# Delta-rule levels with two chunks in one stationary tile, one of them reversed; mixer tiles from a free list; modulation steps placed in VectorE's expected waits

## The chip, the cores and the metric

One NeuronCore of a Trainium2 chip runs the whole program; the other cores are idle. The metric is the device time of one execution in microseconds (us). The kernel before takes 2743.76 us, the median of three runs (2742.51 to 2744.02). About 0.2% (5.5 us) is what a measurement of this kernel can tell from no change.

The engines are named as in the profile: PE is TensorE (PEld its weight loads), DVE is VectorE, ACT is ScalarE, POOL is GpSimd, SP is the engine whose queue issues most DMAs. Each engine takes its instructions in the order in which the program lists them for it.

## The reference: what is computed

One layer of a streaming encoder on 512 prompt frames and 64 sample frames, model width 2048, all in float32. Modulation vectors come from a condition vector (`mod = silu(c) @ w_ada + b_ada`, six vectors of 2048 for prompt and sample). A modulated RMSNorm feeds one input projection; its columns go to two kinds of mixers, four heads of gated linear attention (GLA) and eight heads of gated DeltaNet (GDN); both are exact causal recurrences over the frames. Their gated, normalised outputs are joined and projected back to 2048, then a convolutional feed-forward network follows. What the change touches is the delta rule:

```python
def gdn_step(s, blk):
    '''Gated delta rule: S_t = a_t (I - b_t k_t k_t^T) S_{t-1} + b_t k_t v_t^T, o_t = S_t^T q_t.'''
    ...
    lower = jnp.where(strict, jnp.einsum('bhid,bhjd->bhij', kb, k) * decay, 0.0)
    rhs = jnp.concatenate([v * beta, kb * jnp.exp(big_g)[..., None]], axis=-1)
    sol = lax.linalg.triangular_solve(eye + lower, rhs, left_side=True, lower=True,
                                      unit_diagonal=True)
```

For each head and chunk of frames a unit lower triangular matrix has to be inverted (or solved with). The kernel uses chunks of 128 frames, four per head for the prompt; the 64 sample frames of all eight heads are handled as one more "head" whose four tiles hold two heads each.

## The kernel before, in words

**Stages.** The head normalises x, computes the first two modulation vectors and begins the projection of six of the column blocks. Then, from about 170 us of the span, the mixer stage: `gdn_heads` and `gla_heads` run the remaining 50 column blocks of the input projection one after the other (`in_tile`, 16 products each; a product, `mm6`, is six matmuls of 288 columns, because each float32 operand is split into a high and a low part, `wh`/`wl` and `hh`/`hl`). Then comes the first half of the output projection, over the GDN outputs (16 blocks of 8 products, operands from `load_o`, lines 1515 to 1524), its second half over the GLA outputs (again 16 blocks of 8), then the feed-forward part, which does not concern this change. The split of a weight block into `wh` (ACT) and `wl` (DVE) is emitted with a raised priority.

**Jobs and ticks.** The mixers run as Python generators beside the projection. After each product `tick` (line 624) advances a modelled clock by 0.795 us and lets one job do its next step (`job_step`, line 638). A job yields after a step until the modelled time of its chain of operations (`chain`, kept by `charge`, line 359) is reached, so its matmuls land between the products on PE at a place where their inputs should be there. On DVE and ACT the operations of jobs and of the modulation follow each other in the order of emission (`behind`, line 380); only the weight splits float. The same tick adds 0.72 to a credit and spends it on steps of the late modulation vectors (`ada_blocks`, line 1131): 512 DVE operations of 128x512 (`acc<-aw,ct,acc` and `acc<-xr,ct,acc`), whose weights arrive by 512 KB DMAs; it does so only where the modelled DVE is less than 1 us behind.

**The delta rule, line 189.** `gdn` builds the decay matrices `dl` and `du` (128 x 4 chunks x 128) with ACT and POOL (`affine_select` cuts the triangle), the four matrices `a` (PE, lines 249 to 251), and inverts them: `inverse16` (line 410) first inverts the 16x16 diagonal blocks on DVE, with the blocks moved to 32 lanes and back by DMAs through DRAM (`d0`, `d1`); then the levels 16, 32 and 64 join blocks of that size (lines 266 to 293). A level has two products with a DVE step behind each. `u` and `t` are the inverse and its transpose so far. Every product takes the 128x128 tile of one chunk as the stationary operand and moves 64 columns past it, so a level has four matmuls per product; level 64 uses 64x64 corners:

```python
        for s in (16, 32):
            ...
            for b in range(4):
                T.matmul(ps[:, b * 64:(b + 1) * 64], a[:, b], uh[:, b * nq:(b + 1) * nq], start=True, stop=True)
```

Between levels four transposes renew `t`. After the levels the four chunks are run in order with the state `st`. The GLA levels (`gla`, line 450) already hold two chunks in one stationary tile: the second of a pair is stored with its frames reversed, so that the strict lower triangle of one and the upper triangle of the other share a 128x128 tile, and 128 columns move past it.

**Narrow vectors.** `narrow` (line 1194) computes the decays and gates of all heads for the whole sequence, a chain of short operations on all engines at the start of the mixer stage; cumulative sums are matmuls with triangular constants (`tri`, `tri2`) and last rows with `l127` and `l63`.

**Mixer tiles.** `_MixPool` (line 2348) has 29 tiles of 128x512 in three rings: 17 `m`, 8 `qkv` and 4 `gt`. A new tile takes the oldest of its ring. `fewer` (line 607) holds a GLA job or the sample job back while more than one delta-rule job runs.

A helper records each timed operation, so its line stands for many: in the profile L2272 and L2297 are DVE and ACT operations of jobs and of tasks or splits, L2316 matmuls and L2312 transposes of jobs, L2330 POOL operations; L675 and L677 are the projection's matmuls with `wh` and `wl`.

Of the kernel before, what the change touches and what calls it, by code (L numbers as in the profile page):

```python
# [77 lines left out]
def _shape_constants():  # L78
# [18 lines left out]
    m["l127"] = np.repeat((r == 127)[:, None], P, 1) * 1.0  # L97
    m["l63"] = np.repeat((r == 63)[:, None], P, 1) * 1.0
# [10 lines left out]
NARROW = ("tri", "tri2", "l127", "l63")  # L109


class Kern:
    def __init__(self, tc, ctx, i, o):
# [7 lines left out]
        self.table, self.floating, self.last_of = None, False, {}  # L121
# [22 lines left out]
    def m(self, tag="m", w=512):  # L144
        return self.mp.tile([P, w], F32, tag=tag, name=self.name(tag))

    def m4(self, tag="m"):
        return self.m(tag).rearrange("p (b t) -> p b t", b=4)
# [40 lines left out]
    def gdn(self, qF, kF, x, gain, hcols, gb, s0, s_out, o_put, last_level):  # L189
# [18 lines left out]
        dl, du = self.m4(), self.m4()  # L208
# [5 lines left out]
        self.pool.affine_select(du, du, pattern=[[0, 4], [1, P]], compare_op=ALU.is_ge, fill=0.0, base=0, channel_multiplier=-1)  # L214
        self.pool.affine_select(dl, dl, pattern=[[0, 4], [-1, P]], compare_op=ALU.is_gt, fill=0.0, base=0, channel_multiplier=1)
        if pair:
            self.pool.memset(du[0:64, :, 64:P], 0.0)
# [5 lines left out]
        kT = self.m4()  # L223
# [23 lines left out]
        a = self.m4()  # L247
# [15 lines left out]
        half = lambda x, s, h: flat(x).rearrange("p (n h s) -> p n h s", h=2, s=s)[:, :, h]  # L263
        row4 = lambda x, s: x.rearrange("p (n s) -> p n s", s=s)
        for s in (16, 32):
            uh = half(u, s, 1)
            nq = 64 // s
            ps = self.bank()
            for b in range(4):
                T.matmul(ps[:, b * 64:(b + 1) * 64], a[:, b], uh[:, b * nq:(b + 1) * nq], start=True, stop=True)  # L270
            four = lambda x: x.rearrange("p (b n i) -> p b n i", b=4, i=s)
            V.tensor_tensor(four(pm), four(ps[:, :256]), walk(c[f"p{s}"], 0, (0, 4), (1, nq), (0, s)), op=ALU.mult)
# [4 lines left out]
            V.tensor_tensor(uh, uh, row4(ps[:, :256], s), op=ALU.add)  # L277
            yield from self.hop()
            if s < last_level:
                A.activation(half(t, s, 0), half(self.transpose4(u), s, 0), AF.Copy)  # L280
                yield from self.hop()
        if last_level == 64:
            ps = self.bank()
            for b in range(4):
                T.matmul(ps[:64, b * 64:(b + 1) * 64], a[64:, b, :64], u[64:, b, 64:], start=True, stop=True)
            V.tensor_copy(pm[:64], ps[:64, :256])
            yield from self.hop()
            ps = self.bank()
            for b in range(4):
                T.matmul(ps[:64, b * 64:(b + 1) * 64], t[:64, b, :64], pm[:64, b * 64:(b + 1) * 64], start=True, stop=True)  # L290
            V.tensor_copy(u[:64, :, 64:], ps[:64, :256].rearrange("p (b n) -> p b n", b=4))
            yield from self.hop()
# [46 lines left out]
        if not pair:  # L339
            nc.sync.dma_start(s_out, st)  # L340
# [2053 lines left out]
```

## Time and profile before

| what | value |
|---|---|
| median of three runs | 2743.76 us |
| the profiled execution: its time | 2741.56 us |
| the profiled execution: its span, first to last instruction | 2739.9 us |
| granted PE clock, mean | 0.999 |
| PE busy in the span | 2699.0 us (99%) |
| DVE busy in the span | 2280.0 us (83%) |
| matmuls on PE in the trace | 20404 |
| first matmul of `narrow` | 170.6 us |

The trace is from one execution, 2.2 us faster than the median. A float32 matmul of a job shows as two instructions (two passes), a transpose as one, a projection matmul as one. Matmuls are pipelined, so their busy times overlap, and what one costs is read from the distance between the starts of successive groups in the timeline, not from its duration. In the groups, `out<-in,in` gives the tiles by name without buffer numbers; then the shapes, the count, the busy time, the mean in ns, and the idle time of that engine just before.

### The profile page before, as it was taken

To read this page: it belongs to the slowest core of one execution; us is meant where nothing else is said; L and a number is where in the kernel's file an instruction comes from. 1 tells how busy PE (TensorE), PEld (TensorE's weight loads), DVE (VectorE), ACT (ScalarE), POOL (GpSimd) and SP (SyncE) were. 2 spreads that over 40 slices of the span, in tenths; PEclk is the share of its full clock that TensorE was granted. 3 is DMA by queue.
4 is the path that set the end of the run, shared out by engine and by line. 5 is a ranking of instruction groups with operands and counts; after the bars stand their busy time and mean duration, and the time that the engine had idled before them with its cause. 6 is when DMAs were issued, how large, how long until landed. Compare 5 with 4: busy or idle time off the path is not lost.

```text
span 2739.9 us, 52447 instructions
## 1 busy us (share of the span) xinstructions
PE 2699.0 (99%) x20404; PEld 2632.7 (96%) x20404; DVE 2280.0 (83%) x3691; ACT 1295.7 (47%) x2286; POOL 473.8 (17%) x440
## 2 busy tenths in 40 slices
PE   7999999999999999999999999999999999999998
PEld 5799999999999989999999999999999999999998
DVE  4578887788888898678999999999999976888896
ACT  4245545545644442454545454545454545333453
POOL 0000100001000000001333333333333300000241
PEclk9999999999999999999999999999999999999999
DMA  9985555555565676534464646455655595664762
GB/s 312 344 266 145 152 154 142 148 145 162 168 170 151 177 240 197 148 101 121 138 191 140 188 144 184 149 181 152 179 152 179 151 316 180 209 217 123 238 179 84
DMA packets 645919, 487.61 MB, mean 178 GB/s; under 512 B 66315, under 2 KB 568070, under 8 KB 645670
## 3 DMA queue, kind: packets, MB, share of 16 engines
q1 hardware_dynamic: 632564, 470.77, 57.5%
q10 hardware_dynamic: 13104, 13.47, 1.7%
q8 instruction: 161, 2.64, 0.4%
q14 instruction: 90, 0.72, 0.1%
HBM read 400.12 MB, written 84.04 MB: 177 GB/s over the span
## 4 chain that ended last, share of the span: by engine, by line
PE 89%; DVE 5%; DMA 3%; ACT 1%; issue 1%; SPq 0%; POOL 0%; ACTq 0%; DVEq 0%
PE g L675 19%; PE bank L1785 17%; PE bank L1784 17%; PE bank L1786 17%; PE g L677 9%; PE bank L2316 5%; PE bank L2312 1%; PE bank L675 1%; DVE acc L2297 1%; DVE m L2272 1%; PE bank L904 1%; PE bank L677 1%; DVE wl L1694 0%; DVE wl L2297 0%; PE g L835 0%
## 5 line engine op out<-in xcount | busy, mean ns | idle before, releaser
L1785 PE MATMUL bank<-slot,wh 128*128 128x290 f32 (+1 forms) x3584 | 1067.3, 298 | 0.0
L1784 PE MATMUL bank<-slot,wh 128*128 128x290 f32 (+1 forms) x3584 | 1063.1, 297 | 1.7 <-DVE v L1807 0.6
L1786 PE MATMUL bank<-slot,wl 128*128 128x290 f32 (+1 forms) x3584 | 1060.0, 296 | 1.7 <-DVE wl L1694 1.7
L1786 PEld LDWEIGHTS bank<-slot,wl 128*128 128x128 f32 x3584 | 680.0, 190 | 3.1 <-DVE wl L1694 2.9
L1784 PEld LDWEIGHTS bank<-slot,wh 128*128 128x128 f32 x3584 | 675.4, 188 | 6.3 <-issue 4.7
L1785 PEld LDWEIGHTS bank<-slot,wh 128*128 128x128 f32 x3584 | 676.9, 189 | 0.1
L675 PE MATMUL g<-hh,wh 128*128 128x288 f32 x2048 | 469.5, 310 | 2.2 <-ACT wh L2297 1.3
L1692 ACT ACTIVATE wh<-raw 128x1024 fp32r<-128x1024 f32 (+1 forms) x304 | 280.7, 924 | 348.2 <-PE bank L1785 323.1
L677 PE MATMUL g<-hh,wl 128*128 128x288 f32 x2048 | 439.4, 296 | 2.4 <-DVE wl L1072 2.1
L675 PE MATMUL g<-hl,wh 128*128 128x288 f32 x2048 | 440.6, 296 | 0.9 <-DVE hl L1523 0.6
L1694 DVE TENSOR_TENSOR wl<-raw,wh 128x1024 fp32r<-128x1024 f32 (+1 forms) x304 | 374.6, 1233 | 69.3 <-ACT wh L1692 66.1
L1692 ACT ACTIVATE wh<-s 128x1024 fp32r<-128x1024 f32 (+1 forms) x228 | 210.9, 927 | 298.2 <-PE bank L1785 139.7
L675 PEld LDWEIGHTS g<-hh,wh 128*128 128x128 f32 x2048 | 323.6, 189 | 18.6 <-issue 11.9
L677 PEld LDWEIGHTS g<-hh,wl 128*128 128x128 f32 x2048 | 328.9, 188 | 4.3 <-DVE wl L1072 2.3
L675 PEld LDWEIGHTS g<-hl,wh 128*128 128x128 f32 x2048 | 328.7, 188 | 3.5 <-issue 1.9
L1694 DVE TENSOR_TENSOR wl<-s,wh 128x1024 fp32r<-128x1024 f32 (+1 forms) x228 | 250.4, 1100 | 14.2 <-ACT wh L1692 12.8
L2297 ACT ACTIVATE wh<-raw 128x1024 fp32r<-128x1024 f32 x135 | 143.3, 1062 | 186.0 <-PE g L675 177.6
L2297 DVE SCALAR_TENSOR_TENSOR acc<-aw,ct,acc 128x512 f32<-128x512 f32 x280 | 198.9, 743 | 2.2 <-DMA aw<-in_w_ada_dram 2.2
L1908 POOL TENSOR_TENSOR j<-j,j 128x288 f32<-128x288 f32 (+1 forms) x120 | 186.1, 1557 | 84.0 <-ACT j L1912 81.8
L2297 DVE TENSOR_TENSOR wl<-raw,wh 128x1024 fp32r<-128x1024 f32 x135 | 166.0, 1230 | 16.9 <-ACT wh L2297 14.3
L2297 DVE SCALAR_TENSOR_TENSOR acc<-xr,ct,acc 128x512 f32<-128x512 f32 x200 | 143.0, 744 | 0.0
L1980 DVE TENSOR_TENSOR slot<-bank,slot 128x288 f32<-128x288 f32 x184 | 83.1, 452 | 34.2 <-PE bank L1786 32.9
(330 smaller groups left out, 3274.2 us busy)
## 6 DMA issues: line engine op xcount, KB each, us to landing
raw<-in_w_up_dram SPq DMA_DIRECT2D x176, 512.0 KB
raw<-in_w_in_dram SPq DMA_DIRECT2D x100, 512.0 KB
raw<-in_w_down_dram SPq DMA_DIRECT2D x128, 320.0 KB
slot<-cd SPq DMA_DIRECT2D x140, 288.0 KB
aw<-in_w_ada_dram SPq DMA_DIRECT2D x78, 512.0 KB
cd<-j SPq DMA_DIRECT2D x120, 288.0 KB
xr<-in_w_ada_dram SPq DMA_DIRECT2D x50, 512.0 KB
hraw<-in_w_ada_dram SPq DMA_DIRECT2D x40, 512.0 KB
```

Of the source, the lines that this page charges most:

```text
L675: T.matmul(ps[:, h if bank is None else bank, :n], wh, x[:, h, :n], start=f, stop=False)
L677: T.matmul(ps[:, h if bank is None else bank, :n], wl, ah[:, h, :n], start=False, stop=stop)
L904: T.matmul(ps[32 * k:32 * k + 32, :w], cs[:, k0 + k], got[n][k // per][:, k % per], start=(n == together - 1 + 8 * g + 4 * (1 - mi)), stop ...
L1692: self.nc.scalar.activation(hi, src, AF.Copy)
L1694: self.nc.vector.tensor_tensor(lo, src, hi.bitcast(F32), op=ALU.subtract)
L1784: T.matmul(ps, wh[:, j], hi, start=(c < 3 and j == 0), stop=False, skip_group_check=True)
L1785: T.matmul(ps, wh[:, j], lo, start=False, stop=False, skip_group_check=True)
L1786: T.matmul(ps, wl[:, j], hi, start=False, stop=(j == n - 1), skip_group_check=True)
L1908: minus = lambda out, a, b: G.tensor_tensor(out, a, b, op=ALU.subtract)
L1980: V.tensor_tensor(dst, ps, dst, op=ALU.add)
L2297: r = f(*a, **kw)
L2316: return self.engine.matmul(out, *a, **kw)
```

## The change

The levels now handle a pair of chunks at once. Chunks are stored in the order 0, 2, 1, 3 (the function `slots` that GLA had already used), the chunks in the last two places reversed in time: `gdn_conv` writes q, k and v that way, `narrow` computes its vectors for reversed chunks with reversed triangles (`trir`, `tri2r`, `l0`, `l64`) in more and smaller matmuls, the `affine_select`s become four of half the size, and the outputs are turned back at the end. A reversed chunk's matrix is strictly upper triangular, so the sum of two chunks' matrices (`both`, one new DVE addition) is a full tile without overlap, and `t` holds the two transposed inverses in the same way. A level's product is then two matmuls with 128 moving columns instead of four with 64. Level 64 becomes a level like the others, with the whole 128x128 tile.

`inverse16` inverts the blocks of the reversed chunks in lanes 32 to 47 (lanes 16 to 31 are idle), with three short copies instead of one at its end and one at its start that reverse the lanes, and writes them back with three DMAs instead of one.

Mixer tiles come from one free list of 29; a tile is given back by `drop` when its last reader has been emitted. A job asks for its tiles in advance (`room`) and waits until that many and five more are free; `fewer` is gone. A convolution task waits until the one before has ended (`converting`).

`fill_gap` is called before every timed DVE operation: where the model expects that operation to wait at least 0.5 us for its chain, modulation steps are emitted ahead of it, as far as the credit goes.

```diff
+SPARE = 5
-ADA_BACKLOG, ADA_CREDIT = 1.0, 200.0
+ADA_BACKLOG, ADA_CREDIT, GAP_US = 1.0, 200.0, 0.5
...
+    def room(self, n):
+        while self.mp.spare() < n + SPARE:
+            yield WAIT
+        self.mp.held += n
+        return _Room(n)
...
-        dl, du = self.m4(), self.m4()
+        back, room = room, room or (yield from self.room(5))
+        dl, du = self.m4(room), self.m4(room)
...
-        self.pool.affine_select(du, du, pattern=[[0, 4], [1, P]], compare_op=ALU.is_ge, fill=0.0, base=0, channel_multiplier=-1)
-        self.pool.affine_select(dl, dl, pattern=[[0, 4], [-1, P]], compare_op=ALU.is_gt, fill=0.0, base=0, channel_multiplier=1)
+        for m, op, up in ((du, ALU.is_ge, 1), (dl, ALU.is_gt, -1)):
+            for z, sign in ((slice(0, 2), up), (slice(2, 4), -up)):
+                self.pool.affine_select(m[:, z], m[:, z], pattern=[[0, 2], [sign, P]], compare_op=op, fill=0.0, base=0, channel_multiplier=-sign)
...
-        u, t = yield from self.inverse16(a, gb)
-        pm = dl.rearrange("p b t -> p (b t)")[:, :256]
...
-        for s in (16, 32):
-            uh = half(u, s, 1)
+        pm, both = flat(dl)[:, :256], flat(dl)[:, 256:].rearrange("p (r t) -> p r t", r=2)
+        V.tensor_tensor(both, a[:, 0:2], a[:, 2:4], op=ALU.add)
+        u, t = yield from self.inverse16(a, gb, room)
+        for s in (16, 32, 64):
+            if s > last_level:
+                break
             nq = 64 // s
             ps = self.bank()
-            for b in range(4):
-                T.matmul(ps[:, b * 64:(b + 1) * 64], a[:, b], uh[:, b * nq:(b + 1) * nq], start=True, stop=True)
+            for r in range(2):
+                T.matmul(walk(ps, r * 64, (P, 2), (s, nq), (1, s)), both[:, r],
+                         walk(u, r * P + s, (256 - s, 2), (2 * s, nq), (1, s)), start=True, stop=True)
...
             ps = self.bank()
-            for b in range(4):
-                T.matmul(ps[:, b * 64:(b + 1) * 64], t[:, b], pm[:, b * 64:(b + 1) * 64], start=True, stop=True)
+            for r in range(2):
+                T.matmul(walk(ps, r * 64, (P, 2), (1, 64)), t[:, r], walk(pm, r * 64, (P, 2), (1, 64)), start=True, stop=True)
...
-        if last_level == 64:
-            ps = self.bank()
-            for b in range(4):
-                T.matmul(ps[:64, b * 64:(b + 1) * 64], a[64:, b, :64], u[64:, b, 64:], start=True, stop=True)
...
-        V.tensor_copy(xt, xx.rearrange("p i j -> p j i"))
+        V.tensor_copy(xt[:16], xx[:16].rearrange("p i j -> p j i"))
+        V.tensor_copy(lane[odd, 1], lane[odd, 0][:, ::-1])
+        V.tensor_copy(xx[odd], xt[odd].rearrange("p i j -> p j i"))
         yield from self.until()
-        nc.sync.dma_start(d1.rearrange("w q f -> q w f"), lane)
-        self.moved()
+        nc.sync.dma_start(d1[:, 0:16].rearrange("w q f -> q w f"), lane[:16])
+        for w in range(2):
+            nc.sync.dma_start(d1[w, 16:32], lane[odd, 1 - w])
+        self.moved(3)
...
+    def fill_gap(self):
+        if self.filling or self.floating or self.chain is None:
+            return
+        while self.at_ada >= 1 and self.chain - max(self.free["V"], self.now + HOP_US) >= GAP_US:
+            if not self.ada_step():
+                return
...
-        T.matmul(ps[:, :32], c["tri"], ln[:, :32], start=True, stop=True)
-        T.matmul(ps[:, 32:36], c["tri2"], ln[:, 32:36], start=True, stop=True)
+        for z, n in ((0, ""), (2, "r")):
+            T.matmul(turned(ps, z), c["tri" + n], turned(ln, z), start=True, stop=True)
+            T.matmul(ps[:, 32 + z:34 + z], c["tri2" + n], ln[:, 32 + z:34 + z], start=True, stop=True)
...
+    def drop(self, x):
+        self.free.append(self.place.pop(x.tensor.name))
```

What this moves on the engines is seen in the order of the built programs (a row's name `m_3138` is a mixer tile with its number; `x4` counts equal neighbours). On PE, the first delta-rule job's levels 16 and 32 and its first product of level 64, without the projection's rows between them, before:

```order
L2316 MATMUL bank_3185<-m_3138,m_2702 128x64 x4
L2316 MATMUL bank_3211<-m_2355,m_3137 128x64 x4
L2312 MATMUL bank_3233<-consts_227,m_3138 128x128 x4
L2316 MATMUL bank_3260<-m_3138,m_2702 128x64 x4
L2316 MATMUL bank_3280<-m_2355,m_3137 128x64 x4
L2312 MATMUL bank_3321<-consts_227,m_3138 128x128 x4
L2316 MATMUL bank_3365<-m_3138,m_2702 64x64 x4
```

And now:

```order
L2414 MATMUL bank_3311<-m_3287,m_2377 128x2x64 x2
L2414 MATMUL bank_3351<-m_2377,m_2794 128x2x64 x2
L2410 MATMUL bank_3406<-consts_227,m_3287 128x128 x4
L2414 MATMUL bank_3424<-m_3287,m_2377 128x2x64 x2
L2414 MATMUL bank_3475<-m_2377,m_2794 128x2x64 x2
L2410 MATMUL bank_3498<-consts_227,m_3287 128x128 x4
L2414 MATMUL bank_3531<-m_3287,m_2377 128x2x64 x2
```

Each product has two matmuls of 2x64 columns in place of four of 64; the transposes stay. Over the whole program 144 matmuls of 128x64 and 64 of 64x64 go, and 104 of 128x2x64 come; `narrow` has 17 matmuls instead of 11.

On DVE, around the first level of that job, before:

```order
L2297 TENSOR_TENSOR m_3138<-cm_3077,consts_2028 128x512
L2272 TENSOR_TENSOR m_3147<-bank_3148,m_2731 128x512
L2272 TENSOR_TENSOR m_2732<-bank_3160,m_2732 128x512
L2272 TENSOR_TENSOR qkv_2436<-qkv_2436,m_2442 128x512
L2272 TENSOR_TENSOR m_2355<-bank_3185,consts_2028 128x256
```

And now, with two modulation steps ahead of the level's first DVE step:

```order
L2395 TENSOR_TENSOR m_3287<-cm_3234,consts_2028 128x512
L2395 SCALAR_TENSOR_TENSOR acc_2785<-aw_2818,ct,acc_2785 128x512
L2395 SCALAR_TENSOR_TENSOR acc_2784<-aw_2818,ct,acc_2784 128x512
L2368 TENSOR_TENSOR m_2377<-bank_3311,consts_2028 128x256
L2395 SCALAR_TENSOR_TENSOR acc_2785<-aw_2818,ct,acc_2785 128x512
```

The steps `acc<-aw` that stood behind the level's operations stand ahead of and between them; the last sum of the modulation moves from product 990 of the program to product 952.

On SP, the last writes of the sample frames' GLA outputs (`od_63` to `od_70`, eight of them) and the first loads for the second half of the output projection (`xr<-od`, `raw<-od`). Before, the writes stand among the weights of the first half (`raw<-in_w_out`) and of the modulation (`aw`):

```order
L1341 DMA od_68<-m_12103 256x1x32
L1341 DMA od_70<-m_12103 256x1x32
L582 DMA out_dram<-sl_12535 128x256
L777 DMA raw_12961<-in_w_out_dram 128x8x128
L1520 DMA xr_13352<-od_63 128x576
L1520 DMA xr_13364<-od_65 128x576
L1111 DMA aw_12718<-in_w_ada_dram 128x2x512
L777 DMA raw_13030<-in_w_out_dram 128x8x128
```

And now right ahead of all the loads, the last weights of the first half being issued before them; the row behind is the first block's weights for the second half:

```order
L1431 DMA od_66<-m_12900 256x1x32
L1431 DMA od_68<-m_12900 256x1x32
L1431 DMA od_70<-m_12900 256x1x32
L1616 DMA xr_13374<-od_63 128x576
L1616 DMA raw_13380<-od_64 128x576
L1616 DMA xr_13386<-od_65 128x576
L1616 DMA raw_13392<-od_66 128x576
L1616 DMA raw_13404<-od_68 128x576
L1616 DMA xr_13398<-od_67 128x576
L1616 DMA raw_13416<-od_70 128x576
L1616 DMA xr_13410<-od_69 128x576
L846 DMA raw_13434<-in_w_out_dram 128x8x128
```

The loads are held behind the writes, and the weights behind the loads. The sample job of GLA now ends last: its final transposes stand behind product 995 on PE, with 29 products to go in the first half; before, the last transposes of a mixer job stood behind product 947. On PE the rows ahead of `narrow` and those behind product 995 are the same as before.

More of the change, by code (lines that the diff above doesn't have):

```diff
@@ L302, in gdn @@
         for b in range(4):
-            parts = [(0, P, st)] if not pair else [(0, 64, s0[2 * b]), (64, P, s0[2 * b + 1])]
+            at = b % 2 * 2 + b // 2
+            heads = [2 * b + (n if b % 2 == 0 else 1 - n) for n in range(2)]
+            parts = [(0, P, st)] if not pair else [(0, 64, s0[heads[0]]), (64, P, s0[heads[1]])]
             if parts[0][2] is not None:
@@ L590, in gla @@
             yield
+        for t in ons:
+            self.drop(t, back)
         yield from self.until()
@@ L607, in run_due @@
             self.due.pop(0)[1]()
-    def fewer(self, n):
-        while sum(j[0].__name__ == "gdn" for j in self.jobs) > n:
-            yield WAIT
     def start(self, gen, at=0.0):
@@ L1394, in gdn_samples @@
         x = {}
-        yield from self.fewer(1)
+        room = yield from self.room(8)
         self.put_ready(x, "q", None, 0.0)
@@ L1414, in gla_samples @@
     def gla_samples(self, x):
-        tiles = [self.get_s(n, 256) for n in ("aq", "ak", "ag")]
+        room = yield from self.room(7)
+        tiles = [self.get_s(n, 256, room) for n in ("aq", "ak", "ag")]
         self.moved(3)
@@ L2346, in __getitem__, with __init__ @@
         return st
+class _Room:
+    def __init__(self, n):
+        self.n = n
 class _MixPool:
-    BUFS = {"m": 17, "qkv": 8, "gt": 4}
+    SLOTS = 29
     def __init__(self, tc):
         self.g = tc.tile_pool(name="mp", bufs=1, side="right", reuse_waits="tile")
+        self.free, self.place, self.held = [f"m{n}" for n in range(self.SLOTS)], {}, 0
     def __enter__(self):
```

281 lines of the change are left out of this document (178 added, 103 removed).

## The prediction

> **What bounds the kernel now.** I read the page's busy times and slices first, then the stretches of the stage that changes, then the groups of PE by shape, and last PE's timeline at single groups.
>
> ```profile
> span 2739.9 us, 52447 instructions
> PE 2699.0 (99%) x20404; PEld 2632.7 (96%) x20404; DVE 2280.0 (83%) x3691; ACT 1295.7 (47%) x2286; POOL 473.8 (17%) x440
> PE   7999999999999999999999999999999999999998
> PE 89%; DVE 5%; DMA 3%; ACT 1%; issue 1%; SPq 0%; POOL 0%; ACTq 0%; DVEq 0%
> ```
>
> PE is busy in 99% of the span, and the chain that ended last runs through PE for 89% of it. In stretches (columns: length, then busy time of PE, PEld, DVE, ACT, POOL, the granted clock, DMA share, GB/s), the middle one reaching from the first matmul of `narrow` to the place behind which PE's rows are the same again:
>
> ```profile
> 0.00:170.60 170.60, 149.63 (x1193) 117.51 (x1193) 91.99 (x215) 61.34 (x123) 5.35 (x17) 1.00 0.96 315
> 170.60:1085.00 914.40, 909.05 (x6989) 881.91 (x6989) 777.09 (x1647) 455.40 (x1058) 69.38 (x71) 1.00 0.60 169
> 1085.00:2739.90 1654.90, 1640.33 (x12225) 1633.33 (x12223) 1410.87 (x1830) 778.96 (x1105) 399.06 (x352) 1.00 0.56 169
> ```
>
> In the middle stretch PE idles 914.40 − 909.05 = 5.35 us, at a full clock; DVE is busy for 777.09 us (85%), ACT for 455.40 (50%). So in that stretch the time is what PE's instructions take one behind the other. A job's matmul has no free place there: it stands between two products of the projection, and each us that it takes off PE comes off the end, as long as nothing else takes the place. The first and the last stretch keep their rows on PE, and I let them stand.
>
> **The change part by part.**
>
> *The levels.* These are the groups that go, by shape, and a GLA level for comparison (two instructions for each matmul):
>
> ```profile
> L2316 PE MATMUL bank<-m,m 128*128 128x64 f32 x288 | 36.1, 268 | 0.3 <-DVE m L2297 0.3
> L2316 PE MATMUL bank<-m,m 64*64 64x64 f32 x128 | 10.8, 224 | 0.0
> L2316 PE MATMUL bank<-m 128*128 128x128 f32 x124 | 19.3, 274 | 0.0
> ```
>
> The means of 268 and 274 ns are times from start to end; neighbours overlap, so the price is read between starts. One product of level 32, one of level 64, four plain matmuls of 128 columns, and one GLA level, each with the two rows behind it:
>
> ```profile
> 312.09 1.00 PE L2316 MATMUL bank<-m,m 128*128 128x64 f32 x8
> 312.90 0.51 PE L675 MATMUL g<-hh,wh 128*128 128x288 f32 x2
> 313.24 0.44 PE L675 MATMUL g<-hl,wh 128*128 128x288 f32 x2
> ...
> 319.62 0.68 PE L2316 MATMUL bank<-m,m 64*64 64x64 f32 x8
> 320.23 0.54 PE L675 MATMUL g<-hh,wh 128*128 128x288 f32 x2
> 320.61 0.43 PE L675 MATMUL g<-hl,wh 128*128 128x288 f32 x2
> 320.87 0.43 PE L677 MATMUL g<-hh,wl 128*128 128x288 f32 x2
> ...
> 336.07 1.05 PE L2316 MATMUL bank<-qkv,qkv 128*128 128x128 f32 x8
> 336.87 0.51 PE L675 MATMUL g<-hh,wh 128*128 128x288 f32 x2
> 337.22 0.43 PE L675 MATMUL g<-hl,wh 128*128 128x288 f32 x2
> ...
> 960.87 0.60 PE L2316 MATMUL bank<-m 128*128 128x128 f32 x4
> 961.23 0.51 PE L675 MATMUL g<-hh,wh 128*128 128x288 f32 x2
> 961.58 0.43 PE L675 MATMUL g<-hl,wh 128*128 128x288 f32 x2
> ```
>
> Eight instructions of 64 columns hold PE from 312.09 to 312.90, and the pair behind them needs 0.34 us in place of the 0.26 that an undisturbed pair takes (320.61 to 320.87): 1.15 us up to 313.24. Eight of 128 columns take the same, 336.07 to 337.22 = 1.15. So the price is per instruction, 0.10 us, whether it moves 64 or 128 columns. The GLA level, four instructions of 128 columns in two runs, is what the new product looks like, and it takes 960.87 to 961.58 = 0.71 us. The product of level 64 takes 319.62 to 320.61 = 0.99.
>
> The count: 288 instructions of 128x64 are 36 products (9 jobs, 2 levels, 2 products), 128 of 64x64 are 16 (8 jobs, the sample job has no level 64). All 52 become the GLA form: 36 × (1.15 − 0.71) = 15.8 us, 16 × (0.99 − 0.71) = 4.5 us, together **20.3 us less on PE**. What is new in the form is that the first product of a level fetches its columns in runs of 16, 32 or 64; the old one did too, at 0.10 us an instruction, but there half as many columns were fetched per weight load, so a slower fetch could have been hidden. Bounds: nothing, and for 104 instructions (26 first products of four) a second 0.10 us, 10 us. I take nothing: at level 32 the old form already ran at the price of the plain one.
>
> In the Trainium skill, "TensorE: Matmul & The Clock Gate", section "Back-to-back issue gap", gives an isolated matmul a gap of its columns over 2.4 plus 2.5 ns, so a price by columns. The columns stay the same, 208 × 64 = 104 × 128 = 13,312; by that rule the levels would gain nothing, and it is the third rival below. The rows disagree with it at this size.
>
> *Narrow.* Six more float32 matmuls. Their price here:
>
> ```profile
> 188.62 0.30 PE L1253 MATMUL bank<-cum,xr 128*128 128x36 f32 x2
> 188.76 0.36 PE L1254 MATMUL bank<-cum,xr 128*128 128x4 f32 x2
> 188.98 0.27 PE L1269 MATMUL bank<-consts,cum 128*36 128x128 f32 x1
> ```
>
> Between 0.14 and 0.22 us each, 0.8 to 1.3 us; I take **+1.2**. The rest of `narrow` (about 16 short DVE copies, a constant tile twice as long) lengthens a chain that PE waits for only through `narrow`'s own matmuls, which stand two products later on PE than before; I take nothing, with the bounds of the new waits below.
>
> *DVE, ACT, POOL, DMA of the delta rule.* None of these sets the end; what hides them is PE's 914 us. On DVE each of the nine jobs gains one addition and three short copies and trades the level-64 copies for a masked product and an addition of like size:
>
> ```profile
> L2272 DVE TENSOR_TENSOR m<-m 128x256 f32<-128x256 f32 x56 | 21.0, 417 | 0.0
> L2272 DVE COPY m<-m 32x256 f32<-32x256 f32 x9 | 3.4, 374 | 0.3
> L2297 DVE SCALAR_TENSOR_TENSOR acc<-aw,ct,acc 128x512 f32<-128x512 f32 x280 | 198.9, 743 | 2.2 <-DMA aw<-in_w_ada_dram 2.2
> ```
>
> That is 0.42 + 3 × 0.37 = 1.5 us, for nine jobs 14 us; with 3 us for `narrow`, DVE would have 794 us of work in a stretch of 895, 89% in place of 85%. ACT gets 31 more instructions, POOL 21, SP 18 more small DMAs; all stay far below PE. If the cover went, 17 us of DVE would be the price.
>
> *Modulation steps in the gaps.* The same 512 steps run; those put ahead of a job's operation delay it by up to 0.74 us each if the wait is shorter than the model thought. Queued behind them on DVE are that job's product, the next splits `wl` and, through PE's order, the projection. A step that waits for its own DMA delays all of these; in the trace that came to 2.2 us over 280 steps. PE's waits for DVE in the whole stretch are part of its 5.35 us. So the bounds for new or lost waits in the stage are −5 (all of the old ones go) and +11 (twice as many come on top); I take nothing.
>
> *Mixer tiles, `room`, no `fewer`.* No instruction. Their effect is in the jobs' places: the sample GLA job now ends late, and the second half of the output projection begins 29 products behind its last transposes. A product takes 3 × 0.265 = 0.80 us, so 23 us remain. What has to follow is seen at the same place before (DVE's timeline, then SP's):
>
> ```profile
> 1101.07 0.76 DVE L1523 TENSOR_TENSOR slot<-raw,slot 128x576 fp32r<-128x576 f32 x1 [1.68 <-ACT slot L1522]
> 1101.81 0.94 DVE L2297 SCALAR_TENSOR_TENSOR slot<-g,mod,slot 128x512 f32<-128x512 f32 x2
> 1105.15 1.22 DVE L2297 TENSOR_TENSOR wl<-raw,wh 128x1024 fp32r<-128x1024 f32 x1 [2.40 <-ACT wh L2297]
> 1108.19 0.94 DVE L2297 SCALAR_TENSOR_TENSOR slot<-g,mod,slot 128x512 f32<-128x512 f32 x2 [1.82 <-PE g L677]
> ...
> 1040.03 5.26 SPq L1341 DMA_DIRECT2D od<-m  x8
> ```
>
> Before, the last of the eight operand splits ran at 1101.07 and the first weights were ready at 1106.37, 1.8 us ahead of the first half's end at 1108.19. Now the eight writes take 5.3 us of issue behind the transposes; with about 2 us of ACT and DVE ahead, some 4 us to a first load's split and 8 to 10 for eight splits and the weights (all three estimates from the distances in these rows) that is 19 to 21 us of the 23. I take no wait; the bounds are none and 6 us.
>
> *The sum.* The profiled execution took 2741.6 us: 2741.6 − 20.3 + 1.2 = 2722.5. The median is 2.2 us above the profile, which gives 2724.7; I forecast between the two, **2724 us**.
>
> **The rivals.**
>
> *PE waits take back a part.* DVE is fuller, steps stand ahead of jobs, and the late sample job meets the second half: with 5 to 11 us of new waits from the bounds above, 2729 to 2735. For it speaks that SP's loads now stand right behind the writes; against it that a stage with DVE at 85% left PE idle for only 5.35 of 914 us. Chance 0.17.
>
> *The old waits go too.* These are PE's largest at the start of the output projection, where operands came late:
>
> ```profile
> 998.61 0.52 PE L675 MATMUL g<-hl,wh 128*128 128x288 f32 x2 [0.56 <-DVE hl L1523]
> 1002.00 0.54 PE L675 MATMUL g<-hh,wh 128*128 128x288 f32 x2 [1.35 <-ACT wh L2297]
> ```
>
> The GDN sample job is now done earlier than there, so up to 5 us more may go: 2719. Chance 0.12.
>
> *Columns set the price.* Then only `narrow` counts, 2744 + 1 = 2745, no change. Against it the two 1.15 us above. Chance 0.03; that the pairs are not formed at all is ruled out by the order.
>
> *Slower: the late sample job starves the second half.* One mechanism: writes, loads, splits and weights of the second half stand in one line behind the GLA sample job's last transposes. If that line takes L us, PE waits L − 23. It turns the gain of 19 into a loss of over 5.5 us from L = 23 + 19 + 5.5 = 48 us on, more than twice my estimate; at L = 55 the time is 2737 + 19 = 2756. For it speaks only that nothing else on SP can go ahead. Chance 0.05.
>
> **How the numbers follow.** The forecast's own case, within 3 us of 2724, has 0.63. With the two rivals beside it 0.92 lie below 2738, which is 5.5 us (0.2%, what a measurement of this kernel can tell) under 2743.8; 0.03 lie within, 0.05 above. Since a fuller DVE may cost more than twice the old waits, I move 0.03 from faster to same: faster 0.89, same 0.06, slower 0.05. The range reaches to the rivals on both sides: 2718 to 2735.
>
> **What would show it.** In the profile after: the form 128x128 in jobs on PE with 208 instructions more and none of 64 columns; 0.71 us between starts at a level; some 20 us less PE busy time in the stage and the rest of the span unchanged; PE idle there about 5 us; DVE near 89% of the stage. Wrong would be: a level at 1.15 us (price by columns or runs), idle time of PE ahead of the second half's first matmuls that ends on the operands or `wl` (the late job), or idle time of PE ahead of job matmuls that ends on DVE behind `acc` (the steps in the gaps).

## The result, and the profile after

The changed kernel takes 2729.14 us (median of 6 runs, 2727.45 to 2730.33) against 2743.36 us before (6 runs), a ratio of 0.9945 with a 95% interval of 0.9934 to 0.9956: 14.2 us faster. The forecast was 2724 us in a range of 2718 to 2735.

The page of the kernel after:

```profile
span 2728.2 us, 52233 instructions
PE 2682.6 (98%) x20208; PEld 2620.1 (96%) x20208; DVE 2292.2 (84%) x3747; ACT 1295.6 (47%) x2317; POOL 477.8 (18%) x461
```

For the comparison I cut both spans at the same two instructions of PE: the 97th product of the input projection, shortly before `narrow`, and the first matmul of the output projection's second half. The stretch between them is called the stage below. Columns: length, busy time of PE, PEld, DVE, ACT, POOL, granted clock, DMA share, GB/s; first before, then after.

```profile
0.00:167.12 167.12, 146.15 (x1167) 114.16 (x1168) 90.75 (x210) 59.27 (x121) 5.35 (x17) 1.00 0.96 317
167.12:1114.37 947.25, 941.90 (x7240) 914.06 (x7238) 794.91 (x1678) 467.22 (x1074) 69.38 (x71) 1.00 0.61 171
1114.37:2739.90 1625.53, 1610.96 (x12002) 1604.54 (x12000) 1394.30 (x1804) 769.21 (x1092) 399.06 (x352) 1.00 0.55 168
```

```profile
0.00:170.04 170.04, 148.56 (x1167) 116.39 (x1168) 90.75 (x210) 59.02 (x121) 6.41 (x19) 0.98 0.94 311
170.04:1101.19 931.15, 922.27 (x7044) 898.87 (x7043) 805.19 (x1734) 467.60 (x1104) 74.94 (x90) 1.00 0.60 171
1101.19:2728.20 1627.01, 1611.74 (x12002) 1604.84 (x12000) 1396.21 (x1805) 768.96 (x1092) 396.42 (x352) 1.00 0.56 169
```

The stage is 947.25 − 931.15 = 16.1 us shorter. PE's busy time in it falls by 941.90 − 922.27 = 19.6 us, and its idle time rises from 5.35 to 931.15 − 922.27 = 8.88 us, 3.5 more. The first and the last stretch are 2.9 and 1.5 us longer in this execution. The first one's instructions on PE are those of before, and three runs below that have the old kernel there took 168.3 to 170.6 us for it, so its 2.9 us are no part of the change.

The price of a level, read between starts as in the prediction. These are the two products of a level 64 in the kernel after, the first product of a level 32, whose columns are fetched in runs of 32, and the first product of a level 16, in runs of 16:

```profile
318.72 0.60 PE L2414 MATMUL bank<-m,m 128*128 128x128 f32 x4
319.08 0.51 PE L744 MATMUL g<-hh,wh 128*128 128x288 f32 x2
319.43 0.42 PE L744 MATMUL g<-hl,wh 128*128 128x288 f32 x2
...
320.74 0.61 PE L2414 MATMUL bank<-m,m 128*128 128x128 f32 x4
321.11 0.51 PE L744 MATMUL g<-hh,wh 128*128 128x288 f32 x2
321.45 0.43 PE L744 MATMUL g<-hl,wh 128*128 128x288 f32 x2
...
307.98 0.61 PE L2414 MATMUL bank<-m,m 128*128 128x128 f32 x4
308.35 0.51 PE L744 MATMUL g<-hh,wh 128*128 128x288 f32 x2
308.69 0.43 PE L744 MATMUL g<-hl,wh 128*128 128x288 f32 x2
...
299.74 0.61 PE L2414 MATMUL bank<-m,m 128*128 128x128 f32 x4
300.10 0.51 PE L744 MATMUL g<-hh,wh 128*128 128x288 f32 x2
300.45 0.42 PE L744 MATMUL g<-hl,wh 128*128 128x288 f32 x2
```

From 318.72 to 319.43, from 320.74 to 321.45, from 307.98 to 308.69 and from 299.74 to 300.45 it is 0.71 us each time, with runs of 16 and 32 columns as with runs of 64.

What PE waits for in the stage (us in total, times, longest):

```profile
PE bank L2414 <- DVE m L2368: 3.1, 4, 1.0
PE bank L2414 <- ACT m L2395: 2.0, 1, 2.0
PE bank L2414 <- DVE m L2395: 1.7, 3, 1.0
PE bank L2414 <- DVE sq L2368: 1.4, 2, 0.9
PE g L744 <- DVE kt L2395: 0.7, 1, 0.7
```

Of 8.9 us, 8.2 stand ahead of matmuls of jobs (L2414), and the products of the projection (L744) wait only once. The longest wait lies at the start of the output projection. DVE's timeline there, then PE's row:

```profile
979.35 1.23 DVE L2395 TENSOR_TENSOR wl<-raw,wh 128x1024 fp32r<-128x1024 f32 x1 [1.89 <-ACT wh L2395]
980.50 0.47 DVE L2368 SCALAR_TENSOR_TENSOR sl<-sl,s,bank 128x256 f32<-128x256 f32 x1
980.89 0.75 DVE L2368 TENSOR_TENSOR m<-m,m 128x256 f32<-128x256 f32 x2
...
981.79 0.68 PE L2414 MATMUL bank<-m 128*128 128x128 f32 x4 [1.99 <-ACT m L2395]
```

The split of a weight tile sits at the head of DVE's queue and waits 1.89 us for its half from ACT; behind it stand operations of the GLA jobs, the last of them the product that a level needs, and that level then starts late on PE. (The profile names an operation of ACT as the last releaser; the job's own product on DVE, at 980.89, ends 0.15 us before PE starts.) Before, the waits at this place were those of the projection for its operands and weights, 0.56 and 1.35 us; they are gone, and these stand in their place.

At the start of the second half, DVE's row and SP's,

```profile
1098.24 1.23 DVE L2395 TENSOR_TENSOR wl<-raw,wh 128x1024 fp32r<-128x1024 f32 x1 [2.02 <-ACT wh L2395]
...
1078.34 6.33 SPq L1431 DMA_DIRECT2D od<-m  x8
```

and from the chain of waits the GLA sample job's last transposes:

```profile
1076.97 0.23 PE bank L2410 x2
```

The line of writes, loads, splits and weights behind these transposes ends at 1098.24 + 1.23 = 1099.47, and the half begins at 1101.19: 1.7 us to spare. Before, the same weights were ready at 1106.37 (the `wl` row at 1105.15 in the prediction), and the half began at 1114.37:

```profile
1114.37 0.69 PE L675 MATMUL g<-slot,wh 128*128 128x288 f32 x4
```

So before had 8.0 us to spare, and the late sample job has used up 6.3 of them.

### The profile page after: what moved, and what is told of

Its sections match the earlier page's. It is cut to its first block, busy times and chain, and to the rows that moved or that the text cites. A ratio compares the mean times of both kernels' runs of the same rounds, so it can differ in the third digit from the quotient of the medians.

```text
span 2728.2 us, 52233 instructions
## 1 busy us (share of the span) xinstructions
PE 2682.6 (98%) x20208; PEld 2620.1 (96%) x20208; DVE 2292.2 (84%) x3747; ACT 1295.6 (47%) x2317; POOL 477.8 (18%) x461
## 4 chain that ended last, share of the span: by engine, by line
PE 82%; DVE 8%; DMA 4%; issue 3%; ACT 2%; SPq 0%; POOL 0%; ACTq 0%; DVEq 0%; POOLq 0%
PE g L744 17%; PE bank L1881 16%; PE bank L1880 16%; PE bank L1882 16%; PE g L746 8%; PE bank L2414 4%; DVE wl L1790 2%; PE bank L744 1%; PE bank L2410 1%; DVE m L2368 1%; DVE wl L2395 1%; DMA raw<-in_w_out_dram 1%; PE bank L973 1%; DMA raw<-in_w_in_dram 1%; DVE slot L2076 1%
## 5 line engine op out<-in xcount | busy, mean ns | idle before, releaser
L744 PE MATMUL g<-hh,wh 128*128 128x288 f32 x2048 | 470.1, 310 | 1.6 <-DVE kt L2395 0.7
L744 PE MATMUL g<-hl,wh 128*128 128x288 f32 x2048 | 442.8, 297 | 0.3 <-DVE hl L775 0.2
L744 PEld LDWEIGHTS g<-hh,wh 128*128 128x128 f32 x2048 | 325.5, 189 | 15.9 <-issue 10.4
L744 PEld LDWEIGHTS g<-hl,wh 128*128 128x128 f32 x2048 | 330.6, 189 | 2.7 <-issue 1.9
L2395 DVE SCALAR_TENSOR_TENSOR acc<-aw,ct,acc 128x512 f32<-128x512 f32 x264 | 187.7, 743 | 0.0
L2395 DVE SCALAR_TENSOR_TENSOR acc<-xr,ct,acc 128x512 f32<-128x512 f32 x216 | 154.2, 748 | 0.0
```

What stands on the lines that cost most here:

```text
L744: T.matmul(ps[:, h if bank is None else bank, :n], wh, x[:, h, :n], start=f, stop=False)
L2395: r = f(*a, **kw)
```

## The experiments

Theory A, from the prediction: the time is what PE's instructions take; the levels give 20 us, and the rest of the change costs a few us of PE's waits. Its rivals: the steps in the gaps cause those waits (B), they spare larger ones (C), the first stretch really became longer (D), the columns set the price (E). The numbers of the stage come from each run's own profile, cut at the same two instructions; its idle time is length less PE's busy time, the wait ahead of the second half's first matmul counted in. The expectations count the products from two later than the traces: the 1,024 products of the input projection and the first half are 1022 there, and 988 stands for 990. Runs that are named together ran on the same chip with the kernel before beside them.

**The changed kernel again.** No edit.

> The changed kernel once more, as the yardstick for the three runs beside it. Theory A (PE sets the time: the levels give 20.3 us, narrow costs 1.2, new waits of PE in the projections cost 3.5): 2729 us, 0.9945 to 0.995 of before; PE idles 8 to 10 us in the projections again, at the same places, since the order of instructions is fixed. The 3 us that the first 167 us took longer in the first profile (clock 0.96 to 0.98 there) are that execution's own: they should shrink or go in this one. Rival D (the first stretch really became longer, by the larger constants or by the reordered loads): 3 us again at the same clock or at any.

Measured: 2728.45 us, ratio 0.9944 (0.9931 to 0.9956). PE busy 922.62 us in the stage, idle 10.5. The first stretch took 170.3 us again, so the expectation that its 3 us would shrink missed. In the run of the old kernel with the steps in the gaps, below, it took 170.4, with no part of the levels or constants changed: D falls.

**No steps in the gaps.**

```
-ADA_BACKLOG, ADA_CREDIT, GAP_US = 1.0, 200.0, 0.5
+ADA_BACKLOG, ADA_CREDIT, GAP_US = 1.0, 200.0, 1e9
```

> The changed kernel with no modulation step put ahead of a job's operation (the threshold is set out of reach); they all run at the products' ticks, as before. Theory A (the steps in the gaps neither give nor cost much; the new waits come from the longer work of the jobs on DVE): within 2 us of the changed kernel, 2727 to 2731 us. Rival B (the steps in the gaps cause the new waits): 2725 to 2726 us, PE idle in the projections back near 5 us. Rival C (the steps in the gaps spare waits that the fuller DVE would else bring): 2732 to 2740 us, PE idle in the projections 12 us or more.

Measured: 2747.74 us, 19.3 more than the changed kernel beside it, ratio to before 1.0015 (1.0006 to 1.0024). None of the theories had it so: C had the direction, but the whole gain is gone. PE's waits in the stage and at its end, then the windows row of the stage:

```profile
PE g L744 <- ACT wh L2395: 9.8, 1, 9.8
PE bank L1196 <- DVE acc L2395: 5.3, 1, 5.3
PE bank L2414 <- DVE m L2395: 1.7, 2, 1.4
...
170.20:1116.83 946.63, 924.91 (x7043) 899.06 (x7041) 803.76 (x1735) 467.36 (x1103) 67.27 (x90) 0.99 0.60 168
```

PE idles 946.63 − 924.91 = 21.7 us here; 15.7 of them are two waits and a short one between them, at one place, and the 6.0 elsewhere are fewer than the 10.5 of the changed kernel beside it. PE's, ACT's and SP's timelines at that place:

```profile
1104.04 1.73 PE L1196 MATMUL bank<-acc,consts 128*32 128x256 f32 x8 [5.30 <-DVE acc L2395]
1106.31 0.69 PE L2410 MATMUL bank<-consts,rows 128*128 128x128 f32 x2 [0.55 <-ACT rows L2395]
1116.83 1.33 PE L744 MATMUL g<-slot,wh 128*128 128x288 f32 x4 [9.84 <-ACT wh L2395]
...
1105.87 0.39 ACT L2395 ACTIVATE rows<-bank 128x256 f32<-128x256 f32 x1 [25.45 <-PE bank L1196]
1106.15 0.68 ACT L1618 ACTIVATE slot<-xr 128x576 fp32r<-128x576 f32 x1
...
1086.02 11.39 SPq L1180 DMA_DIRECT2D aw<-in_w_ada_dram  x4
...
1110.15 1.06 SPq L846 DMA_DIRECT2D raw<-in_w_out_dram  x2
```

The wait costs more than its length. These are the windows behind the start of the second half, here and in the first profile of the changed kernel:

```profile
1116.83:1121.00 4.17, 4.17 (x17) 3.89 (x18) 2.43 (x2) 1.06 (x1) 0.00 (x0) 0.53 1.20 290
1101.19:1105.00 3.81, 3.81 (x31) 3.81 (x30) 1.35 (x3) 0.00 (x0) 0.00 (x0) 1.00 1.20 291
```

The granted clock is 0.53 here, and the first three products take 1.91, 1.44 and 1.06 us in place of 0.79 each, 2.0 us more. Of the 16.6 us between the spans of this execution and the changed kernel's beside it, 11.2 are idle time of PE in the stage, 2.3 are busy time there, and 3.2 lie behind it.

The modulation is not done when the first half ends. In the code the second half begins only when all blocks are summed (a loop runs the rest of them out). PE waits for the last block's accumulator (5.30 us); ACT's copy `rows` of that block is queued ahead of the operand splits and holds them up (25.45 us idle); SP issues the last modulation loads ahead of the second half's first weights, which are asked for at 1110.15 and set PE free at 1116.83. What hid the 17 us of DVE work in the prediction, PE's 914 us, does not hide it: the steps have to be done by a fixed point, and the jobs' longer work takes their places on DVE.

**The levels split again, everything else as changed.**

```
+                for h in range(2):
+                    T.matmul(walk(ps, r * 64 + h * P, (s, nq), (1, s)), both[:, r],
+                             walk(u, r * P + s + h * (256 - s), (2 * s, nq), (1, s)), start=True, stop=True)
...
+                    T.matmul(walk(ps, r * 64 + h * P, (1, 64)), t[:, r], walk(pm, r * 64 + h * P, (1, 64)), start=True, stop=True)
```

> The changed kernel, but each matmul of a delta-rule level is issued as two of 64 columns, so that a product of a level is 8 instructions again, with the same columns in all. Theory A (a price per instruction, 0.44 us for the four more of each of the 52 products): 22.9 us more than the changed kernel, 2750 to 2753 us, slower than before by 7 to 9 us; 1.15 us between starts at a level. Rival E (columns set the price, and the gain came from the free list and the steps in the gaps): 2729 us, no change, 0.71 us at a level.

Measured: 2749.06 us, 20.6 more than the changed kernel; ratio to before 1.0023 (1.0014 to 1.0032). The group of split levels, and the stage:

```profile
L2416 PE MATMUL bank<-m,m 128*128 128x64 f32 x416 | 52.2, 268 | 1.2 <-DVE m L2397 1.0 <-DVE rq L2397 0.2
...
169.72:1120.56 950.84, 943.99 (x7251) 920.76 (x7250) 808.90 (x1734) 471.34 (x1107) 83.71 (x90) 1.00 0.60 171
```

416 instructions in place of 208, with the same columns, make PE 943.99 − 922.62 = 21.4 us busier, 0.103 us an instruction. E falls; the time is 1 us under A's 2750 to 2753. In the Trainium skill, "TensorE: Matmul & The Clock Gate", section "Back-to-back issue gap", the gap of an isolated matmul goes by its columns, while in a stream of weight loads and matmuls both set the spacing. These rows are such a stream, with a weight load for every matmul instruction (7250 and 7251), and the price is not by the columns.

**The kernel before with steps in the gaps.** The threshold, `ada_step` and `fill_gap` of the change, and nothing else of it.

```
+            if self.key == "V":
+                self.k.fill_gap()
```

> The kernel before with the modulation steps in the gaps added and nothing else changed. Theory A: within 2 us of before, 2742 to 2745 us. Rival B: 3 to 5 us slower, 2746 to 2749 us, with PE waits for DVE behind modulation steps. Rival C: 2 to 4 us faster, 2739 to 2741 us, PE idle in the projections below 4 us.

Measured: 2748.75 us, ratio 1.002 (1.0011 to 1.0029): 5.6 us slower. The stage:

```profile
170.38:1123.95 953.57, 944.52 (x7240) 915.73 (x7238) 795.33 (x1678) 468.77 (x1074) 71.48 (x71) 1.00 0.60 170
```

PE idles 953.57 − 944.52 = 9.1 us in the stage, 3.7 more than before. So by themselves the steps in the gaps cost, as B had it (that its waits stand behind modulation steps was not followed up); in the changed kernel they are worth 19 us. That made theory G: they matter only because they end the modulation ahead of the second half.

**The end of the modulation brought about in another way.**

```
-ADA_BACKLOG, ADA_CREDIT, GAP_US = 1.0, 200.0, 0.5
+ADA_BACKLOG, ADA_CREDIT, GAP_US = 1.2, 200.0, 1e9
```

> The changed kernel with no step in the gaps, but at the products' ticks a modulation step may now be issued while the model sees up to 1.2 us of work ahead on DVE, in place of 1.0. By the order the last modulation block is summed behind product 976 of the projections' first 1022; in the run without gap steps the last two came behind 994 and at the very end. Theory G (what the gap steps do is to end the modulation before the second half of the output projection; any way to end it in time will do, and without gap steps PE waits about 3 us less): 2724 to 2728 us, the time from the end of the first half on as in the changed kernel (1616 us). Rival F (the second half was late for another reason, the sample job that ends late): 2740 us or more, with PE waits at the second half's first weights again.

Measured: 2728.26 us, ratio 0.9943 (0.9930 to 0.9957). The stage:

```profile
169.94:1100.60 930.66, 920.93 (x7043) 897.21 (x7042) 804.32 (x1734) 468.21 (x1104) 71.49 (x90) 1.00 0.61 173
```

The second half starts without a wait, and F falls; it is an end in time that counts. The other half of the expectation missed: PE idles 9.7 us in the stage though no step stands in a gap.

**Gaps that hold a whole step.** The threshold at 1.0 us in place of 0.5.

> The changed kernel with steps only in gaps of 1.0 us or more, so that a step of 0.74 us fits whole where the model is right. The last block is summed behind product 957. Theory G with the waits put down to steps that overrun their gaps: PE idles 5 to 7 us in the projections in place of 9 to 10, 2725 to 2727 us. Rival H (the new waits come from a fuller DVE and wrong gap estimates of any size): 2728 to 2731 us.

Measured: 2726.26 us, ratio 0.9933 (0.9920 to 0.9945). PE idles 6.6 us in the stage. A threshold of 2.0 us was to run beside it (2724 to 2727 us by theory G) and has no time: with it the kernel leaves a ninth of the elements of one tile, `od8_71`, without a number, and why is open. A threshold changes the order of the whole program, so what the kernel computes has to be settled anew for each.

**The kernel before with more work on DVE.**

```
+            for _ in range(2):
+                V.tensor_scalar_mul(pm, pm, 1.0)
```

> The kernel before with two operations of DVE more at each of its two lower levels (a tile times 1.0, 128 x 256; 36 operations for nine jobs, 0.35 to 0.42 us each, 13 to 15 us), about what the change adds to DVE. The value computed is the same. By the order the last modulation block is now summed behind product 1021, at the end of the first half, in place of 988. Theory G (there is no room for the added DVE work ahead of the second half, though DVE is busy for only 85% of the stage): 10 to 20 us slower than before, 2753 to 2763 us, with PE waits for the last block's sum and for the second half's first weights. Rival I (PE's 914 us hide it, as the forecast of the change put it): 2743 to 2746 us.

Measured: 2760.5 us, ratio 1.0057 (1.0044 to 1.0070), 16.6 us slower. The group that was added, the first two waits of PE in the stage and at its end, and the stage:

```profile
L2274 DVE TENSOR_SCALAR m<-m 128x256 f32<-128x256 f32 x36 | 10.6, 294 | 1.1
...
PE g L677 <- ACT wh L2299: 10.7, 2, 10.3
PE bank L2318 <- DVE sl L2274: 1.5, 1, 1.5
...
170.59:1129.66 959.07, 942.44 (x7239) 913.67 (x7237) 803.33 (x1715) 467.27 (x1072) 57.19 (x71) 1.00 0.59 166
```

10.6 us of DVE work, in a stage where DVE was busy for 84% of the time (794.91 of 947.25 us), cost 16.6 us. In this execution 10.3 us are one wait for the second half's first weights, and the first three products behind it take 2.4 us longer, at a granted clock of 0.50. Rival I, which is the prediction's own step, falls; G holds, in a kernel that has nothing of the change, but for its wait for the last block's sum: that sum came behind product 1,023 of 1,024 and kept PE from nothing.

**Four thresholds side by side.** The changed kernel, then the threshold at 1.0 and at 3.0 us, then 1.5 us with ticks up to 1.2.

> The changed kernel beside the three below on the same chip: 2727 to 2730 us.

> The threshold of 1.0 us again, this time beside the changed kernel. If steps that overrun their gaps caused part of the new waits, it is 2 to 4 us faster than the changed kernel again, 2725 to 2727 us; if the difference was the chip's, they agree within 1 us.

> Steps only in gaps of 3.0 us or more. By the order the last block is summed behind product 992 of 1022, the jobs' last matmul before transposes stands behind product 962 in place of 985. If every step that is put ahead of a job costs PE, this has fewest of them and is fastest, 2723 to 2726 us, with PE idle 5 to 6 us in the projections. If waits come with whatever brings the modulation to its end in time, 2726 to 2729 us.

> Gaps of 1.5 us or more and ticks up to 1.2 us of work ahead; the last block is summed behind product 931, the earliest of all. If an early end of the modulation is worth something by itself: 2723 to 2726 us. If only an end in time counts, and steps ahead of jobs cost: 2727 to 2730 us.

| run | median us | ratio to before | PE busy in the stage | idle |
|---|---|---|---|---|
| changed kernel | 2731.80 | 0.9960 (0.9948 to 0.9973) | 922.50 | 10.9 |
| threshold 1.0 | 2725.89 | 0.9943 (0.9931 to 0.9956) | 921.26 | 6.3 |
| threshold 3.0 | 2727.38 | 0.9946 (0.9932 to 0.9960) | 920.63 | 8.6 |
| 1.5, ticks to 1.2 | 2723.02 | 0.9930 (0.9918 to 0.9943) | 920.82 | 5.1 |

The rows behind the first and the last of them:

```profile
170.06:1103.46 933.40, 922.50 (x7043) 898.96 (x7042) 804.33 (x1734) 467.23 (x1104) 74.87 (x90) 1.00 0.60 171
```

```profile
169.74:1095.61 925.87, 920.82 (x7043) 897.36 (x7042) 805.15 (x1734) 470.40 (x1107) 80.14 (x90) 1.00 0.62 175
```

PE's busy time differs by 2 us at most; most of the difference between the times is PE's idle time (5.8 of the 8.8 us between the first row and the last). It does not follow the number of steps in the gaps: the threshold of 3.0 us, with fewer of them, idles more than that of 1.0, and no gap steps at all with ticks to 1.2 idle 9.7. So that steps overrun their gaps is not shown to be the cause. That it is the place where each job's operations fall among weight splits and steps fits the one wait that was followed up above, and is argued, not shown. The last version is faster than both kernels: 8.8 us faster than the changed one beside it, by intervals that do not meet, 7.5 of them in the stage (933.40 against 925.87).

**Its settings in the kernel before.** The run with steps in the gaps, at 1.5 us and ticks up to 1.2.

> The kernel before with the settings of the fastest run: steps in gaps of 1.5 us or more, ticks up to 1.2 us of work ahead; nothing of the levels or tiles changed. The last modulation block is summed behind product 901 in place of 988. If the settings spare PE waits only where the jobs' fuller DVE work made them, before gains nothing: 2741 to 2745 us, PE idle in the projections 5 to 7 us. If an early end of the modulation is worth something in any kernel: 2737 to 2740 us.

Measured: 2742.44 us against 2742.43, ratio 0.9999 (0.9990 to 1.0008). The stage took 945.54 us with PE busy for 942.40, so PE idled 3.1 us, less than the 5 to 7 expected. In the kernel before, an early end of the modulation is worth nothing that can be measured. The fastest run above fell in the range given there for an early end that is worth something by itself, so for the changed kernel this stays open.

## Why the prediction was right or wrong

- **The bound and the levels: right.** 20.3 us less for the levels and 1.2 more for `narrow` made 19.1 us less on PE; busy time fell by 19.6 (19.3 and 19.4 in the other two executions of the changed kernel; executions with the same instructions on PE differ by up to 2 us in it, so the agreement is no finer than that). 0.71 us between starts came out as forecast, and the split showed that it is the number of instructions. `narrow` was not measured alone.
- **The slow fetch of runs: right to leave out.** Runs of 16, 32 and 64 columns cost the same.
- **DVE's work: the step that failed.** "None of these sets the end; what hides them is PE's 914 us." DVE's busy time in the stage rose by 10.3 us (794.91 to 805.19), less than the 17 forecast, to 86% of the stage in place of 89%, and PE's time was no cover for it: the modulation had to share it and to end by the second half. Without the steps in the gaps this costs 19.3 us, more than the 17 us that the prediction named as the price without cover.
- **The modulation steps in the gaps: costed at nothing, worth 19.3 us.** "The same 512 steps run" is true, but they run earlier: in the traces the last block's sum came behind product 952 of the first 1,024 in the changed kernel, behind 990 before, and behind the last one without the gap steps. The time came out near the forecast because I had left out both this gain and the loss that it makes good; that is luck.
- **The new waits: mis-sized.** I took nothing between −5 and +11 us; the three executions of the changed kernel had 3.5, 5.2 and 5.6 us more idle time on PE than before. With that term 2724 becomes 2728 to 2730. The medians of the changed kernel, 2729.14, 2728.45 and 2731.80, lie at the rival "PE waits take back a part" (2729 to 2735) or within 1 us of it, not at the forecast's own case within 3 us of 2724.
- **The second half's start: right that PE does not wait, from a row that was misread.** The line behind the GLA sample job's last transposes took 1099.47 − 1077.20 = 22.3 us (estimated 19 to 21 of 23), and 1.7 us remained. The 1108.19 that the prediction takes for the first half's end before is the sum of a block on DVE, one block earlier; the half ended at 1114.37, with 8.0 us to spare and not 1.8. So the late job came nearer to starving the half than the prediction could see. The slow rival, that this line starves the half, did not come. (In its sum for 55 us, 2756 is 2724 + 32; no row gives the 2737 and the 19 that stand there.) The same half can be starved by the modulation instead, for 10 us, as two runs showed; no rival named that.
- **"The old waits go too": half right.** The operands' waits at the start of the output projection went, but a GLA job's wait of 2.0 us took their place.
- **Not settled:** which placement causes which single wait, and what the free list and `room` do by themselves; they were not run apart from the levels.

## What to carry to other kernels

Background work with a due time uses the spare time of its engine: before adding to that engine, ask when the background work now ends and how far the addition pushes that, and not only how busy the engine is. Where small matmuls are bound by their number, putting two in one stationary tile can pay in full on the engine that sets the end: here PE's busy time fell by 19.6 us where 19.1 were forecast. After such a change the thresholds of the planner are worth another look: here they gave another 8.8 us, and gave the old kernel nothing.

## What the runs showed of the hardware

A float32 matmul instruction of a level, with its own 128x128 stationary tile, cost 0.10 us whether it moved 64 or 128 columns (0.103 us for each one that the split added), and the fetch of 128 columns in runs of 16 or 32 cost no more than in runs of 64. A price that goes by the stationary tile fits this: in the Trainium skill, "TensorE: Matmul & The Clock Gate", section "LDWEIGHTS (loading the stationary operand)", loading one takes its columns over 1.2, which is 107 ns for 128. For the old level 64, with 64 columns, that rule gives 53 ns, and the rows of before show (320.23 − 319.62) / 8 = 76 ns. So as a price of an instruction the rule comes near at 128 columns and not at 64. The loads of before themselves (PEld):

```profile
L2316 PEld LDWEIGHTS bank<-m,m 64*64 64x64 f32 x128 | 8.6, 134 | 2.6 <-issue 2.0 <-PE g L675 0.3 <-DVE m L2272 0.2
L2316 PEld LDWEIGHTS bank<-m,m 128*128 128x128 f32 x372 | 50.0, 191 | 2.0 <-DVE sl L2272 0.7 <-DVE m L2297 0.5
```

From start to end a load lasts 134 ns with 64 columns and 191 with 128. The 57 ns between them are near the 53 that the rule gives for 64 columns more; but loads overlap, and the price of an instruction falls by only 25 ns, from 101 to 76. That the load sets the price is argued, not shown.

Behind a wait of PE of about 10 us the granted clock was 0.53 for the first 4.2 us in the run without gap steps, and 0.50 for the first 3.3 us in the run of before with more work on DVE; that added 2.0 and 2.4 us to the first three products.

The granted clock of the first 168 us was 1.00 in one execution and 0.98 or 0.99 in the others, whichever kernel ran, and that stretch took up to 3.5 us longer in them. That the clock is all of this is not shown.
